# Two waits moved in a two-sweep hybrid decoder block: the attention projection's results and the next sweep's norms

## The chip, the cores and the metric

The kernel runs on one core of a Trainium2 chip. The metric is device time in microseconds (us) of one execution. The core has five engines that work side by side and wait for each other through semaphores: TensorE (PE: matmuls, with its weight loads PEld), VectorE (DVE), ScalarE (ACT), GpSimd (POOL), and SyncE (SP), whose queue issues the transfers. Each engine works its own instructions in the order in which they stand in the program.

## The reference

A decoder block over 2048 tokens of width 1024, in float32:

```python
h = rmsnorm(x, norm_g)
proj = h @ w_in          # glu_in, conv_gate, q, k, v, attn_gate, merge_logits
c = silu(layernorm(depthwise_conv31(a * sigmoid(b))))       # a, b = glu_in
y_conv = (c * silu(conv_gate)) @ w_conv_out
a = sliding_window_attention(rope(q), rope(k), v, sinks)    # window 128, 16 heads, 4 kv heads
y_attn = (a * silu(attn_gate)) @ w_attn_out
merged = sigmoid(m_conv) * y_conv + sigmoid(m_attn) * y_attn
out = rmsnorm(x + merged @ w_out, final_norm_g)
```

## The kernel before

The tokens are worked in two sweeps of 1024, and each product of a sweep in two halves of 512 tokens. The tiles have channels on the 128 partitions and tokens along the row, so a product of 128 output channels and one half is eight steps over the input channels. Each float32 operand is split into a high and a low part, and each step is three matmuls (high x high, high x low, low x high), 24 matmuls for a half. A line over all steps, `Line.run`, calls the products (items) one after another. An item yields after each step, and `spend` then moves a planned clock `t` on and puts in other work that is due: background operations (`bg`, one every `every` us of planned time), and chains (`late`), which are generators that yield the planned us until they may go on. TensorE's order is the order in which the program writes its matmuls. The other engines' orders are set by a scheduler from dependences and priorities, with what is written earlier or at high priority first.

In a sweep the products are, in this order: the inputs of the convolution (`gb`, `ga`), k, v and q, the gates (`ag`, `cg`, `ma`, `mc`, spilled to DRAM), with the attention's small matmuls in between, then:

- `ya`, the attention projection, 8 items of 128 channels (e = 0 to 7) with two halves. A result stands in a bank of PSUM, out of a pool of three banks (`mm_ps`), and VectorE empties it: `ev` in `ya_item` loads the merge gate (`lma`) and multiplies it into the tile `mp`. The tile `mp[e]` lies in the slot `C[e]`, in which the convolution's result `cv[e]` stood. So the operations that read `cv[e]` have to be written before: these are the gated tiles, `u_op(e, h)`, which load the gate (`lcg`), multiply it with `cv[e]` on VectorE (lcg<-lcg,cv, L815), cast the high part on ScalarE (uT<-lcg, L301) and subtract it for the low part on VectorE (uT<-lcg,uT, L234). There are 16 of them, two per channel block. They are background operations, and `u_op` notes each in `stored`.
- `yc`, the convolution's projection, 8 items that read all sixteen uT. VectorE and GpSimd add `mp` to its result, and the sum is split into `mT`.
- `o`, the output product, 16 blocks (n = 0, 1 for the halves of the output channels, b = 0 to 7 for 128 tokens). Beside it, in sweep 0, `prepare` makes the next sweep's input. It squares rows of x on ScalarE (`next_square`), and after blocks 3 and 7 starts a chain, `next_norm`, for the norm of one half of 512 tokens. Its first part makes n10 (for half 0) or n11 (half 1): a root (n11rt), a diagonal tile (n11d) and its high and low part (n11h on ScalarE, n11l on VectorE). After a planned wait, two matmuls by a tile of ones spread the norm over the partitions (n10ms, n11ms), and ScalarE copies the result to `rs`. `next_h` multiplies it with the loaded x (xh) and splits that into `hT`, the input of sweep 1.

The weights of each item come in two parts of four steps (raw_ya, with the number of the item and of the part, 20 and 21 for e = 2). They are cast on ScalarE (whi_ya), GpSimd subtracts for the low part (wlo_ya), and SP stores that to DRAM (d_lo). Four buffers hold each kind.

Of the kernel before, what the change touches and what calls it, by code (L numbers as in the profile page):

```python
# [53 lines left out]
def hybrid_block(ctx: ExitStack, tc: tile.TileContext, x, xt, par_d, w_in, w_conv, sinks, w_attn, w_out,  # L54
# [26 lines left out]
    def slot(tag, shape, dt, name):  # L81
        n = int(np.prod(shape[1:]))
        full = 1024 + P if tag in WIDE else 1024
        t = slots.tile([P, full], dt, tag=tag, name=name)
        v = t[:, 0:n]
        if len(shape) == 3:
            v = v.rearrange("p (a b) -> p a b", b=shape[2])
        elif len(shape) == 4:
            v = v.rearrange("p (a b c) -> p a b c", b=shape[2], c=shape[3])
        return v  # L90

    def t2k(name, dt=F32):
        return work.tile([P, TH], dt, tag="t2k", name=name, bufs=5)
# [65 lines left out]
    class Line:  # L159
# [46 lines left out]
        def finish(self):  # L206
            self.finish_bg()
            while self.late:
                self.t = max(self.t, min(c[0] for c in self.late))
                self.spend(0.1)  # L210

        def run(self, items):


            held = None
            for item in items:
                item[0]()
                if held is not None:
                    for us in held[1]():
                        self.spend(us)  # L220
                held = item
            for us in held[1]():
                self.spend(us)
            self.finish()

    line = Line()
# [6 lines left out]
    def split_lo(out_, full, hi, eng):  # L233
        eng.tensor_tensor(out=out_, in0=full, in1=f(hi), op=ALU.subtract)  # L234
# [38 lines left out]
    def small_bank(name):  # L273
        return tp_ps.tile([P, 4, P], F32, tag="tp", name=name).rearrange("p a b -> p (a b)")

    def project(src, rhs, name, evac, halves=(0, 1), small=False):

        got = {}

        def prefetch():  # L280
            got["w"] = load_w(src, name)

        def blocks():
            for half in halves:
                if small:
                    ps = small_bank(f"mm_{name}{half}")
                else:
                    ps = mm_ps.tile([P, TH], F32, tag="mm", name=f"mm_{name}{half}")
                for k in range(KC):
                    product(ps, got["w"][0](k), rhs(k, half), k)  # L290
                    if k == KC - 1:
                        with tc.high_priority(offset=PRIO):
                            evac(half, ps)
                    if half == halves[-1] and k % 4 == 3:
                        got["w"][1](k // 4)
                    yield 3 * MM_US

        return prefetch, blocks, (src, name, evac)
# [20 lines left out]
    def norm_chain(ss, bank, rs, wait, name):  # L319

        rt = work.tile([P, 2, 4], F32, tag="rt", name=f"{name}rt")
        act.activation(out=rt[:, 0], in_=ss, func=AF.Sqrt, bias=eps, scale=1.0 / D)
        dve.reciprocal(out=rt[:, 1], in_=rt[:, 0])
        dg = t2k(f"{name}d").rearrange("p (b t) -> p b t", t=P)
        dve.tensor_tensor(out=dg, in0=ident.unsqueeze(1).broadcast_to([P, 4, P]),
                          in1=rt[:, 1].unsqueeze(2).broadcast_to([P, 4, P]), op=ALU.mult)
        dg = dg.rearrange("p b t -> p (b t)")
        hi, lo = (t2k(f"{name}{p}", F32R) for p in "hl")
        act.copy(hi, dg)
        split_lo(lo, dg, hi, dve)  # L330
        yield 0.0, wait
        ms = bank()
        for i, part in enumerate((hi, lo)):
            pe.matmul(out=ms, lhsT=ones, rhs=part, start=(i == 0), stop=(i == 1))
        act.activation(out=rs, in_=ms, func=AF.Copy, scale=float(D))
        yield 2 * MM_US, 0.0
# [132 lines left out]
    def sweep(s):  # L469
# [59 lines left out]
        stored = set()  # L529
# [11 lines left out]
        def load_gate(kind, e, half):  # L541
            g = t2k(f"l{kind}{s}_{e}_{half}")
            nc.sync.dma_start(out=g, in_=spill[kind][s * KC + e, :, half * TH:(half + 1) * TH])
            return g
# [297 lines left out]
        def start_u():  # L842
            uT.extend(make_tiles(HT, h, f"uT{s}_") for h in range(2))
# [37 lines left out]
        def ya_item(e, first):  # L881
            def ev(half, ps):
                if half == 0:
                    if ("u", e, 1) not in stored:
                        line.finish()
                    mp[e] = slot(C[e], [P, T], F32, f"mp{s}_{e}")
                g = load_gate("ma", e, half)
                dve.tensor_tensor(out=mp[e][:, half * TH:(half + 1) * TH], in0=ps, in1=g, op=ALU.mult)  # L888

            prefetch, blocks, _ = project(w_attn[e], lambda k, half: aT[half][k],  # L890
                                       f"ya{s}_{e}", ev)
            if not first:
                return prefetch, blocks

            def first_blocks():
                start_u()
                if None in aT[0] + aT[1]:
                    line.finish()
                yield from blocks()

            return prefetch, first_blocks
# [26 lines left out]
        nx = {}  # L928
# [13 lines left out]
        def next_norm(half):  # L942
            ss = nx["ss"]
            dve.tensor_tensor(out=ss[:, 2], in0=ss[:, 0], in1=ss[:, 1], op=ALU.add)
            return norm_chain(ss[:, 2], lambda: small_bank(f"n{s + 1}{half}ms"), nx["rs"][:, half], 6.0,
                              f"n{s + 1}{half}")

        def next_h(half, k):
# [4 lines left out]
        def prepare(n, b):  # L953
            i = n * NB + b
            if i < 8:
                next_square(i)
            if i in (3, 7):
                line.start(next_norm(i // 4))
            if 6 <= i < 10:
                for k in range(2):  # L960
                    next_h(0, 2 * (i - 6) + k)
            if i == 11:
                ht[1] = make_tiles(h_tags[s + 1], 1, f"hT{s + 1}_")
            if 11 <= i < 15:
                for k in range(2):
                    next_h(1, 2 * (i - 11) + k)
# [121 lines left out]
```

## Time and profile before

| | |
|---|---|
| median of 3 runs | 2035.56 us (2034.6 to 2036.1) |
| the profiled execution, its own time | 2036.56 us |
| its span, from the first to the last instruction | 2034.8 us |
| mean granted TensorE clock | 0.994 of full speed |
| busy: TensorE, VectorE, ScalarE, GpSimd | 1999.4, 1337.9, 1031.3, 395.9 us |
| sweep 0: first ya matmul, first matmul of sweep 1 | 748.92, 1034.28 us |

The profile is of one execution. Its rows give start and duration in us, the engine, the line of the kernel, the instruction with output and inputs (buffer numbers left out), how many of them follow each other, and in brackets how long the engine was idle before and which engine or transfer ended that. In a list of waits stand the sum, the number of times and the longest. The granted clock is TensorE's, as a share of full speed.

### The profile page before, as it was taken

The page shows a single profiled execution, that of the slowest core. Times are in us where ns is not written, and L with a number is a line of the kernel's source. Part 1 is how long each engine was busy: PE and PEld are TensorE (multiplying, and loading weights), DVE is VectorE, ACT ScalarE, POOL GpSimd, SP SyncE. Part 2 cuts the span into 40 slices and gives each one's busy share as a digit, 9 for nine tenths or more (in the row PEclk, how much of TensorE's full clock was granted, in tenths as well). Part 3 has the DMA queues.
Part 4 walks back from the last instruction along what each step waited for, and adds up shares of the span by engine and source line. Part 5 has one row for each costly group of instructions (what it writes and reads, how often), then busy time and mean ns, then how long its engine had stood idle before and what let it go on. Part 6 is the DMA issues. An engine that isn't in the chain of part 4 may idle for free.

```text
span 2034.8 us, 27254 instructions
## 1 busy us (share of the span) xinstructions
PE 1999.4 (98%) x9136; PEld 1658.5 (82%) x9136; DVE 1337.9 (66%) x1931; ACT 1031.3 (51%) x2271; POOL 395.9 (19%) x328
## 2 busy tenths in 40 slices
PE   8999999999999997999999999999999999999998
PEld 6788888888888886888788888888888888888887
DVE  6998879988993363123749587699888924441324
ACT  7321677767677362123523225777777774621222
POOL 0344233233323222341001120110111010001200
PEclk9999999999999998999999999999999999999999
DMA  8445645555556746446543466455555578474432
GB/s 292 145 140 177 219 154 171 172 175 171 160 189 225 254 161 206 145 145 222 176 146 133 148 195 197 153 183 173 173 165 173 169 231 267 163 234 147 149 115 83
DMA packets 268699, 361.13 MB, mean 177 GB/s; under 512 B 28432, under 2 KB 126864, under 8 KB 268560
## 3 DMA queue, kind: packets, MB, share of 16 engines
q1 hardware_dynamic: 268560, 359.40, 54.1%
q8 instruction: 72, 1.18, 0.2%
q14 instruction: 67, 0.55, 0.1%
HBM read 239.75 MB, written 119.54 MB: 177 GB/s over the span
## 4 chain that ended last, share of the span: by engine, by line
PE 51%; DVE 1%; DMA 0%; issue 0%; ACT 0%; DVEq 0%; ACTq 0%
PE o L1012 6%; PE mm_ma L271 4%; PE mm_cg L271 4%; PE mm_ag L271 4%; PE mm_gb L271 4%; PE mm_ga L271 4%; PE mm_mc L271 4%; PE mm_yc L271 4%; PE mm_ya L271 4%; PE mm_q_a L271 2%; PE mm_q_b L271 2%; PE sc L668 2%; PE ov L718 1%; PE mm_v L271 1%; PE tpp L698 1%; PE mm_kb L271 1%
## 5 line engine op out<-in xcount | busy, mean ns | idle before, releaser
L492 DVE SCALAR_TENSOR_TENSOR acc<-glu,par,acc 128x1024 f32<-128x1024 f32 x464 | 596.1, 1285 | 6.1
L1012 PE MATMUL o<-wo,mT 128*128 128x512 f32 x768 | 177.4, 393 | 0.0
L271 PE MATMUL mm_ya<-aT,whi_ya 128*128 128x512 f32 x512 | 158.9, 392 | 12.5 <-DVE mp L888 12.5
L1012 PEld LDWEIGHTS o<-wo,mT 128*128 128x128 f32 x768 | 146.2, 190 | 30.7
L271 PE MATMUL mm_ma<-hT,whi_ma 128*128 128x512 f32 x512 | 159.7, 393 | 0.0
L271 PE MATMUL mm_cg<-hT,whi_cg 128*128 128x512 f32 x512 | 159.7, 393 | 0.0
L271 PE MATMUL mm_ag<-hT,whi_ag 128*128 128x512 f32 x512 | 159.4, 393 | 0.0
L271 PE MATMUL mm_mc<-hT,whi_mc 128*128 128x512 f32 x512 | 157.9, 390 | 0.0
L271 PE MATMUL mm_yc<-uT,whi_yc 128*128 128x512 f32 x512 | 157.6, 389 | 0.0
L709 POOL TENSOR_SCALAR_AFFINE_SELECT pc<-pt 128x1024 fp32r<-128x1024 f32 x60 | 65.6, 1094 | 422.5 <-DVE pt L234 413.7
L271 PE MATMUL mm_gb<-hT,whi_gb 128*128 128x512 f32 x448 | 139.2, 392 | 0.0
L271 PE MATMUL mm_ga<-hT,whi_ga 128*128 128x512 f32 x448 | 139.2, 392 | 0.0
L271 PEld LDWEIGHTS mm_ya<-aT,whi_ya 128*128 128x128 f32 x512 | 96.8, 189 | 33.0 <-DVE mp L888 12.9
L271 PEld LDWEIGHTS mm_yc<-uT,whi_yc 128*128 128x128 f32 x512 | 96.1, 188 | 20.0
L271 PEld LDWEIGHTS mm_mc<-hT,whi_mc 128*128 128x128 f32 x512 | 96.0, 188 | 20.0
L271 PEld LDWEIGHTS mm_ag<-hT,whi_ag 128*128 128x128 f32 x512 | 94.2, 188 | 18.2
L271 PEld LDWEIGHTS mm_ma<-hT,whi_ma 128*128 128x128 f32 x512 | 94.1, 188 | 18.2
L271 PEld LDWEIGHTS mm_cg<-hT,whi_cg 128*128 128x128 f32 x512 | 94.0, 188 | 18.2
L688 ACT ACTIVATE ss<-ss,st 128x128 f32<-128x128 f32 x256 | 99.7, 390 | 11.3 <-DVE st L683 10.7
L271 PE MATMUL mm_ya<-aT,wlo_ya 128*128 128x512 f32 x256 | 100.1, 391 | 0.0
L271 PE MATMUL mm_ma<-hT,wlo_ma 128*128 128x512 f32 x256 | 99.9, 390 | 0.0
L271 PE MATMUL mm_cg<-hT,wlo_cg 128*128 128x512 f32 x256 | 99.9, 390 | 0.0
(449 smaller groups left out, 4255.6 us busy)
## 6 DMA issues: line engine op xcount, KB each, us to landing
qk<-d_q SPq DMA_DIRECT2D x256, 64.0 KB, 2.2
d_a<-ss SPq DMA_DIRECT2D x128, 128.0 KB, 1.9
aT<-d_a SPq DMA_DIRECT2D x32, 512.0 KB, 5.9
qk<-d_k SPq DMA_DIRECT2D x240, 64.0 KB, 2.0
raw_ag<-in_w_in_dram SPq DMA_DIRECT2D x32, 256.0 KB, 3.7
d_ag<-ag SPq DMA_DIRECT2D x32, 256.0 KB, 2.2
ss<-d_ag SPq DMA_DIRECT2D x64, 128.0 KB, 2.6
raw_cg<-in_w_in_dram SPq DMA_DIRECT2D x32, 256.0 KB, 3.5
```

The source lines that it names most:

```text
L271: pe.matmul(out=ps, lhsT=a, rhs=b, start=(k == 0 and i == 0), stop=(k == KC - 1 and i == 2))
L492: dve.scalar_tensor_tensor(out=to, in0=glu[c][:, j:j + T], scalar=tap(c, j), in1=acc[c], op0=ALU.mult, op1=ALU.add)
L668: pe.matmul(out=o, lhsT=q[:, h, :], rhs=r, start=(j == 0), stop=(j == 1))
L688: act.activation(out=sb[:, h, :], in_=sb[:, h, :], func=AF.Exp, scale=SCALE, bias=ngm[:, h:h + 1], accum_out=den[:, h:h + 1])
L698: pe.transpose(out=tpp[:, h, :], in_=sb[:, h, :], identity=ident)
L709: pool.affine_select(out=pc, in_=f(pt), pattern=[[0, 2], [0, GQ], [1, P]], compare_op=ALU.is_ge, fill=0.0, base=0, channel_multiplier=-1)
L718: pe.matmul(out=ov, lhsT=vv, rhs=pp[:, i % 2], start=(i == 0), stop=(i == nm - 1))
L1012: pe.matmul(out=ps, lhsT=a[:, c0:c0 + P], rhs=r, start=(k == 0 and i == 0), stop=(k == KC - 1 and i == 2))
```

## The change

There are two edits. In `ya_item`, when the first half of block e is to be emptied and block e's own second gated tile is not written yet, the kernel before writes all background operations and lets all chains end (`finish`). The kernel after writes background operations only until that tile is there (`until`). And the planned wait of the norm chain of the next sweep's halves is 12 us in place of 6.

```diff
         def finish(self):
             self.finish_bg()
             while self.late:
                 self.t = max(self.t, min(c[0] for c in self.late))
                 self.spend(0.1)
+
+        def until(self, ok):
+            while not ok():
+                if self.bg:
+                    self.bg.popleft()()
+                else:
+                    self.t = max(self.t, min(c[0] for c in self.late))
+                    self.spend(0.1)
...
             def ev(half, ps):
                 if half == 0:
-                    if ("u", e, 1) not in stored:
-                        line.finish()
+                    line.until(lambda: ("u", e, 1) in stored)
                     mp[e] = slot(C[e], [P, T], F32, f"mp{s}_{e}")
...
-            return norm_chain(ss[:, 2], lambda: small_bank(f"n{s + 1}{half}ms"), nx["rs"][:, half], 6.0,
+            return norm_chain(ss[:, 2], lambda: small_bank(f"n{s + 1}{half}ms"), nx["rs"][:, half], 12.0,
                               f"n{s + 1}{half}")
```

The lines behind the first edit stand 8 numbers further on in the kernel after, and 7 behind the second. No instruction is added or taken away on any engine. The ya stage of sweep 1 has the same order in both.

VectorE, in sweep 0, where ya begins; a name like uT_1_6 is half 1 of gated tile 6, mp_0<-mm_ya_00 the result of half 0 of item 0. Before, the end of the gated tiles:

```order
L815 TENSOR_TENSOR lcg_6_1_7244<-lcg_6_1_7244,cv_6_5881 128x512
L234 TENSOR_TENSOR uT_0_6_7140<-lcg_6_0_7239,uT_0_6_7140 128x512
L815 TENSOR_TENSOR lcg_7_0_7249<-lcg_7_0_7249,cv_7_6565 128x512
L234 TENSOR_TENSOR uT_1_6_7148<-lcg_6_1_7244,uT_1_6_7148 128x512
L815 TENSOR_TENSOR lcg_7_1_7254<-lcg_7_1_7254,cv_7_6565 128x512
L234 TENSOR_TENSOR uT_0_7_7141<-lcg_7_0_7249,uT_0_7_7141 128x512
L888 TENSOR_TENSOR mp_0_7259<-mm_ya_00_7150,lma_0_0_7260 128x512
L888 TENSOR_TENSOR mp_0_7259<-mm_ya_01_7263,lma_0_1_7289 128x512
L234 TENSOR_TENSOR uT_1_7_7149<-lcg_7_1_7254,uT_1_7_7149 128x512
L888 TENSOR_TENSOR mp_1_7330<-mm_ya_10_7305,lma_1_0_7331 128x512
```

After, the beginning of the gated tiles:

```order
L823 TENSOR_TENSOR lcg_0_1_7184<-lcg_0_1_7184,cv_0_1313 128x512
L242 TENSOR_TENSOR uT_1_0_7142<-lcg_0_1_7184,uT_1_0_7142 128x512
L895 TENSOR_TENSOR mp_0_7189<-mm_ya_00_7150,lma_0_0_7190 128x512
L823 TENSOR_TENSOR lcg_1_0_7197<-lcg_1_0_7197,cv_1_2036 128x512
L823 TENSOR_TENSOR lcg_1_1_7208<-lcg_1_1_7208,cv_1_2036 128x512
L823 TENSOR_TENSOR lcg_2_0_7220<-lcg_2_0_7220,cv_2_2785 128x512
L895 TENSOR_TENSOR mp_0_7189<-mm_ya_01_7193,lma_0_1_7234 128x512
L242 TENSOR_TENSOR uT_0_0_7134<-lcg_0_0_7173,uT_0_0_7134 128x512
```

The mp of the first half moved from behind 31 of the 32 operations of the gated tiles to behind three of them. After the second mp stand 9 operations of gated tiles, then the third mp, then 7, the fourth, 8, the fifth, 2, the sixth.

ScalarE, at the same place, after the change; whi_ya_30 and whi_ya_31 are the two parts of item 3's weights, which stand behind all uT casts before:

```order
L309 CAST uT_1_2_7144<-lcg_2_1_7238 128x512
L309 CAST uT_0_3_7137<-lcg_3_0_7262 128x512
L309 CAST uT_1_3_7145<-lcg_3_1_7273 128x512
L257 CAST whi_ya_30_7350<-raw_ya_30_7349 128x512
L309 CAST uT_0_4_7138<-lcg_4_0_7287 128x512
L309 CAST uT_1_4_7146<-lcg_4_1_7303 128x512
L309 CAST uT_0_5_7139<-lcg_5_0_7314 128x512
L257 CAST whi_ya_31_7356<-raw_ya_31_7355 128x512
```

The weight casts moved between the casts of the gated tiles.

TensorE, in sweep 0's output product, second half of the channels (o_1_1 is n = 1, block 1). Before:

```order
L1012 MATMUL o_1_0_8851<-wo_1_7_8817,mT_0_7_7834 128x512 x3
L1012 MATMUL o_1_1_8895<-wo_1_0_8761,mT_0_0_7827 128x512 x3
L334 MATMUL n11ms<-n11h,ones 128x512
L334 MATMUL n11ms<-n11l,ones 128x512
L1012 MATMUL o_1_1_8895<-wo_1_1_8769,mT_0_1_7828 128x512 x3
```

After:

```order
L1019 MATMUL o_1_1_8895<-wo_1_7_8817,mT_0_7_7834 128x512 x3
L1019 MATMUL o_1_2_8939<-wo_1_0_8761,mT_0_0_7827 128x512 x3
L1019 MATMUL o_1_2_8939<-wo_1_1_8769,mT_0_1_7828 128x512 x3
L342 MATMUL n11ms<-n11h,ones 128x512
L342 MATMUL n11ms<-n11l,ones 128x512
L1019 MATMUL o_1_2_8939<-wo_1_2_8777,mT_0_2_7829 128x512 x3
```

The pair n11ms moved back by nine steps of o, 27 matmuls. The pair n10ms moved by the same number, from behind the first step of block 5 (n = 0) to behind the second step of block 6.

## The prediction

> **What bounds the kernel now.** I read the page's head first, then the waits of TensorE, then the chain that ended last, and then the timelines around the waits.
>
> ```profile
> span 2034.8 us, 27254 instructions
> ...
> PE 1999.4 (98%) x9136; PEld 1658.5 (82%) x9136; DVE 1337.9 (66%) x1931; ACT 1031.3 (51%) x2271; POOL 395.9 (19%) x328
> ```
>
> TensorE is the bound. Only time in which it stands still, or runs slowly, can be won. The waits of TensorE, sorted by size:
>
> ```profile
> PE mm_ya L271 <- DVE mp L888: 12.5, 1, 12.5
> PE mm_gb L271 <- ACT w L249: 6.9, 1, 6.9
> PE n11ms L334 <- ACT n11h L329: 3.9, 1, 3.9
> ...
> PE n11ms L334 <- DVE n11l L234: 0.7, 1, 0.7
> ...
> PE n10ms L334 <- DVE n10l L234: 0.2, 1, 0.2
> ```
>
> The wait of 6.9 is the start of the kernel, which the change leaves alone. The other four rows, 12.5 + 3.9 + 0.7 + 0.2 = 17.3 us, belong to the two edits. No row names a product of sweep 1. Idle time is not the whole price, though. The chain that ended last gives the pace of sweep 1, and the start of its first product:
>
> ```profile
> 1034.28 10.88 PE mm_gb L271 x48
> ...
> 1767.02 87.04 PE mm_ya L271 x384
> 1854.06 87.04 PE mm_yc L271 x384
> 1941.10 87.05 PE o L1012 x384
> ```
>
> In sweep 1 ya, yc and o take 87.04 + 87.04 + 87.05 = 261.13 us for 1152 matmuls, 0.2267 each, 5.44 us for a half of 24. Sweep 0 runs the same 1152 and the four of the two norms (0.91 us) between its first ya matmul and 1034.28. TensorE's timeline has that first matmul and the long wait:
>
> ```profile
> 748.92 0.61 PE L271 MATMUL mm_ya<-aT,whi_ya 128*128 128x512 f32 x2
> ...
> 765.01 0.39 PE L271 MATMUL mm_ya<-aT,wlo_ya 128*128 128x512 f32 x1
> 777.91 1.22 PE L271 MATMUL mm_ya<-aT,whi_ya 128*128 128x512 f32 x2 [12.51 <-DVE mp L888]
> ...
> 782.27 0.62 PE L271 MATMUL mm_ya<-aT,whi_ya 128*128 128x512 f32 x2
> ```
>
> So sweep 0 needs 1034.28 - 748.92 = 285.36 us where 261.13 + 0.91 = 262.04 would do: 23.3 us are lost, 6 more than the idle rows say. The stretches show why (columns: TensorE, its weight loads, VectorE, ScalarE, GpSimd busy, granted clock, DMA share, GB/s):
>
> ```profile
> 765.24:777.91 12.67, 0.16 (x1) 0.00 (x1) 12.50 (x17) 6.07 (x11) 3.14 (x2) 0.59 0.81 258
> 777.91:782.50 4.59, 4.59 (x14) 3.65 (x14) 1.93 (x3) 0.22 (x1) 0.00 (x0) 0.65 0.92 309
> 782.50:850.50 68.00, 68.00 (x301) 56.31 (x300) 8.32 (x13) 8.08 (x14) 16.75 (x13) 1.00 0.44 151
> ...
> 988.00:994.20 6.20, 1.55 (x5) 0.77 (x4) 6.14 (x13) 4.40 (x10) 0.00 (x0) 0.89 0.92 329
> 994.20:1001.00 6.80, 6.80 (x20) 5.33 (x19) 5.02 (x8) 1.91 (x4) 0.00 (x0) 0.60 0.47 152
> 1001.00:1034.28 33.28, 33.28 (x148) 27.57 (x147) 20.32 (x35) 12.41 (x29) 0.35 (x2) 1.00 0.45 156
> ```
>
> After each long wait the granted clock is 0.65 and 0.60 for some microseconds, then 1.00. TensorE is busy there and yet behind. From 777.91 to 782.27 it starts 12 matmuls in 4.36 us instead of 2.72.
>
> **The change part by part.** It removes and adds no instruction. It moves VectorE, ScalarE and SP instructions in sweep 0's ya stage, and two pairs of matmuls in sweep 0's output stage.
>
> First edit, ya in sweep 0. There are three banks for products, so half number i+3 of ya cannot start before the mp product has emptied the bank of half i. In the order before, the mp of half 0 stands behind all gated tiles but one. VectorE's timeline:
>
> ```profile
> 751.74 1.89 DVE L815 TENSOR_TENSOR lcg<-lcg,cv 128x512 f32<-128x512 f32 x3
> 754.11 1.29 DVE L234 TENSOR_TENSOR uT<-lcg,uT 128x512 fp32r<-128x512 f32 x2 [0.49 <-ACT uT L301]
> ...
> 758.02 4.09 DVE L234 TENSOR_TENSOR uT<-lcg,uT 128x512 fp32r<-128x512 f32 x3
> ...
> 775.85 0.68 DVE L815 TENSOR_TENSOR lcg<-lcg,cv 128x512 f32<-128x512 f32 x1
> 776.45 0.68 DVE L234 TENSOR_TENSOR uT<-lcg,uT 128x512 fp32r<-128x512 f32 x1
> 777.17 0.69 DVE L888 TENSOR_TENSOR mp<-mm_ya,lma 128x512 f32<-128x512 f32 x1
> ```
>
> Half 0 was complete at 748.92 + 5.44 = 754.36, and its mp ran at 777.17. Half 3 was due at 748.92 + 3 x 5.44 = 765.24 and started at 777.91: 12.67 us, and 4.36 - 2.72 = 1.64 at the low clock, 14.3 in all.
>
> The new order puts the mp of half 0 behind three instructions, and the others between groups of gated tiles. I walk it at 0.60 us a step (775.85 to 776.45). Dear steps: uT beside GpSimd's wlo took 4.09 for three, 2.2 more than 1.8, and GpSimd's rows coincide with them:
>
> ```profile
> 758.51 3.05 POOL L234 TENSOR_TENSOR wlo_ya<-raw_ya,whi_ya 128x512 fp32r<-128x512 f32 x2 [18.46 <-ACT whi_ya L249]
> 766.65 3.14 POOL L234 TENSOR_TENSOR wlo_ya<-raw_ya,whi_ya 128x512 fp32r<-128x512 f32 x2 [5.09 <-DMA d_lo<-wlo_ya]
> ```
>
> Each pair of wlo thus costs VectorE up to 2.2 us, and three pairs fall into the stretch. Half i ends at 754.36 + 5.44 i, and I add 0.2 for the signal. mp 0: 754.6 + 0.6 = 755.2, due 765.24. Three lcg, then mp 1, which waits for its half: 760.0 + 0.6 = 760.6, due 770.68. Nine steps, 5.4 (with two pairs 9.8), and 0.6 for mp 2 itself: 766.6 to 771.0, due 776.12. Seven steps, 4.2 (with half a pair 5.3): mp 3 at 771.5 to 776.9, due 781.56. Eight steps, 4.8 (5.9): mp 4 at 776.9 to 783.4, due 787.00. Two steps: mp 5 at 782.4 to 785.2, due 792.44. Every mp is in time, by 3.6 us in the dear column and by 9.5 or more in the cheap one. TensorE does not wait: 14.3 us won.
>
> What the new waits hold up: VectorE now stands before each mp until its half is done, with lcg and uT queued behind. The last uT comes at some 778 to 785 instead of 779.6. Its reader is yc, due at 748.92 + 87.04 = 835.96: no cost, 50 us of cover. On ScalarE the weight casts stand between uT casts. The cast of block 3's first weights follows uT_1_3, some 767 to 772. It could not be before half 3 is half done anyway, 768.0, as it was at 782.28 before:
>
> ```profile
> 782.28 0.62 ACT L249 CAST whi_ya<-raw_ya 128x512 fp32r<-128x512 f32 x1 [5.10 <-PE mm_ya L271]
> ```
>
> With GpSimd's 1.5 us behind it the weights are there by 774 at the latest, due 781.56. On SP the loads of lma move ahead, and two stores of wlo (blocks 2) stand before the loads of the last eight lcg. They wait for GpSimd until some 766. I cost this at nothing, since the eight lcg are due from 769 on. If that cover is gone, an mp is late by what exceeds 3.6 us.
>
> In sweep 1 the order of ya is the same in both programs: nothing.
>
> Second edit, the norms. Each pair now stands 27 matmuls further back, 27 x 0.2267 = 6.12 us. The rows of n11:
>
> ```profile
> 983.67 4.70 PE L1012 MATMUL o<-wo,mT 128*128 128x512 f32 x20
> 992.30 0.50 PE L334 MATMUL n11ms<-n11h,ones 128*128 128x512 f32 x1 [3.93 <-ACT n11h L329]
> 993.52 0.79 PE L334 MATMUL n11ms<-n11l,ones 128*128 128x512 f32 x1 [0.72 <-DVE n11l L234]
> ```
>
> and VectorE's last step before them:
>
> ```profile
> 992.79 0.68 DVE L234 TENSOR_TENSOR n11l<-n11d,n11h 128x512 fp32r<-128x512 f32 x1
> ```
>
> TensorE was there at 983.67 + 20 x 0.2267 = 988.2. It will come at 994.3 on the same scale, and n11l is complete at 993.47: 0.8 us to spare. VectorE's new order also takes one hT (about 0.7) from ahead of n11l. n10 waited 0.2 and gets 6.12: to spare. What goes is the rest of the loss, 23.3 - 14.3 = 9.0 us: 0.2 + 3.9 + 0.7 idle, and 4.2 of low clock and slow steps around them (20 recorded matmuls in 6.80 us instead of 4.5, and the pair itself).
>
> What a late norm makes late is the next sweep's hT, half 1:
>
> ```profile
> 995.34 0.59 ACT L335 ACTIVATE rs<-n11ms 128x512 f32<-128x512 f32 x1
> ...
> 1015.84 0.73 DVE L340 SCALAR_TENSOR_TENSOR hT<-xh,par,hT 128x512 fp32r<-128x512 f32 x1
> ```
>
> From rs to the last hT it takes 21.2 us. The new rs comes at 994.3 + 1.4 = 995.7 on the scale that had n11 at 988.2, so hT is complete at 1016.9. On that scale gb of sweep 1 begins 8.1 earlier than 1034.28, at about 1026, and its half 1 at 1031.6: 15 us of cover.
>
> The price of the low clock could also be taken from the Trainium skill, page "TensorE: Matmul & The Clock Gate", Part 1: after an idle window of about 3.4 us the array runs at half rate and needs about 3.4 us of activity to be released. By it each of the two long waits would cost about 1.7 us more, and the sum would be 17.3 + 3.4 = 20.7, a time near 2015. The trace agrees at ya (1.64), and at n11, with 0.60 over 6.8 us, it shows more than one such window. I keep the trace's sum.
>
> Sum: -14.3 - 9.0 = -23.3, and I give back 0.3 for short waits that may stay at n10 and n11. The profiled execution took 2036.56 (span 2034.8, 1.7 around it), so it would be 2013.5. The median of the runs, 2035.56, lies 1.0 lower: 2012.5.
>
> **The rivals.** First, n11 stays partly. Its 0.8 us to spare is thin, and xh and xs loads stand ahead of it on VectorE. If they are 1 to 5 us late, 0.2 to 4 us come back, with the low clock up to 7: 2013 to 2019.5. For it speaks the thin margin, against it the hT that is gone from ahead.
>
> Second, VectorE stays behind TensorE in ya: at 1.36 a step (4.09 for three) the 13 uT between mp 1 and mp 4 cost 9.9 us more than at 0.60, and mp 4 ends at 786.8, just in time. Any lcg load that is late behind SP's stores, by the 3 us that such a load takes or by twice that, then stops TensorE for 3 to 6 us: 2015 to 2019. For it speaks that VectorE has some 28 us of work in 30 us there, against it that only six wlo run in the stretch.
>
> Third, slower: sweep 1 waits for hT, since rs of half 1 comes later against the start of sweep 1. It decides once that chain of 21.2 us grows by more than its 15 us of cover. It must grow by 38 us to eat the gain too. At 42 us more the time would be 2040. Nothing in the rows stretches it so far.
>
> Fourth, the change does nothing that counts, 2035.5: the order of sweep 0 speaks against it.
>
> **How the numbers follow.** Both waits gone 0.80 (2011 to 2014), n11 partly 0.08, ya partly 0.08, slower 0.02, nothing 0.02. The range 2010.5 to 2017 takes the first case, with 1.5 us of spread between runs (2034.6 to 2036.1), and most of the next two. About 0.2%, 4 us, is what a measurement here can tell from no change: faster 0.96, same 0.02, slower 0.02.
>
> **What would show it.** Right: no wait of mm_ya for mp and none of n11ms among TensorE's waits; mp of half 0 some 6 us after the first ya matmul; granted clock 1.00 from 749 to the end; gb of sweep 1 starting near 1011; last uT before 786. Wrong: a wait of mm_ya for mp or for wlo_ya of blocks 2 to 4, a wait of n11ms of over 1 us, or a first wait of sweep 1's gb for hT.

## The result, and the profile after

The kernel after takes 2012.85 us, the median of 4 runs (2012.16 to 2013.28), the kernel before beside it 2035.54 (2034.60 to 2036.10). The ratio is 0.9889, with a 95% interval from 0.9872 to 0.9906: 22.7 us less, where 2012.5 was forecast. The head of the page:

```profile
span 2011.6 us, 27250 instructions
...
PE 1993.1 (99%) x9136; PEld 1654.8 (82%) x9136; DVE 1337.0 (66%) x1931; ACT 1031.6 (51%) x2271; POOL 396.8 (20%) x328
```

The span is 23.2 us shorter, and TensorE is busy for only 6.3 us less: 17 us were idle time, the rest was slow time that counted as busy. Each engine has the same number of instructions as before. Of the waits of TensorE the four rows of before are gone, and none stands in their place. The two longest are now the start of the kernel and one in the attention:

```profile
PE mm_gb L279 <- ACT w L257: 7.2, 1, 7.2
PE sc L676 <- DVE pt L242: 1.3, 1, 1.3
```

The chain that ended last is now TensorE alone from ya to the next sweep:

```profile
748.92 87.04 PE mm_ya L279 x384
835.96 87.04 PE mm_yc L279 x384
923.00 34.01 PE o L1019 x150
957.00 0.46 PE n10ms L342 x2
957.46 21.81 PE o L1019 x96
979.27 0.46 PE n11ms L342 x2
979.73 31.32 PE o L1019 x138
1011.05 10.88 PE mm_gb L279 x48
```

Sweep 0 now has sweep 1's pace, 87.04 us for ya. The stretches of after (columns as before) cover ya, the place of the old wait, and the output product:

```profile
748.75:835.79 87.04, 87.04 (x385) 72.07 (x384) 36.22 (x50) 28.30 (x42) 23.77 (x17) 1.00 0.59 200
765.24:777.91 12.67, 12.67 (x57) 10.49 (x57) 11.80 (x17) 5.37 (x9) 3.09 (x2) 1.00 0.82 268
...
922.83:1011.05 88.22, 88.22 (x390) 72.98 (x389) 50.49 (x87) 44.14 (x106) 1.64 (x3) 1.00 0.59 203
```

Where the kernel before stood for 12.5 us, TensorE works all 12.67 us with the clock at 1.00. VectorE works 11.80 there, 12.50 before: the same work, in another order. The two starts that split the loss of before are these, from TensorE's timeline of before:

```profile
850.27 0.62 PE L271 MATMUL mm_yc<-uT,whi_yc 128*128 128x512 f32 x2
...
937.32 7.87 PE L1012 MATMUL o<-wo,mT 128*128 128x512 f32 x34
```

Before, ya took 850.27 - 748.92 = 101.35 us, after 87.04: 14.31 won. The output product took 1034.28 - 937.32 = 96.96, after 88.22: 8.74 won. Together 23.05.

VectorE's mp, in the timeline of after:

```profile
754.67 0.69 DVE L895 TENSOR_TENSOR mp<-mm_ya,lma 128x512 f32<-128x512 f32 x1
...
759.83 0.69 DVE L895 TENSOR_TENSOR mp<-mm_ya,lma 128x512 f32<-128x512 f32 x1 [1.21 <-PE mm_ya L279]
760.44 3.58 DVE L242 TENSOR_TENSOR uT<-lcg,uT 128x512 fp32r<-128x512 f32 x4
765.97 1.34 DVE L823 TENSOR_TENSOR lcg<-lcg,cv 128x512 f32<-128x512 f32 x2 [1.94 <-DMA lcg<-d_cg]
...
769.26 0.69 DVE L895 TENSOR_TENSOR mp<-mm_ya,lma 128x512 f32<-128x512 f32 x1
...
775.34 0.68 DVE L895 TENSOR_TENSOR mp<-mm_ya,lma 128x512 f32<-128x512 f32 x1
...
781.75 0.69 DVE L895 TENSOR_TENSOR mp<-mm_ya,lma 128x512 f32<-128x512 f32 x1
782.36 1.28 DVE L242 TENSOR_TENSOR uT<-lcg,uT 128x512 fp32r<-128x512 f32 x2
783.56 0.68 DVE L895 TENSOR_TENSOR mp<-mm_ya,lma 128x512 f32<-128x512 f32 x1
787.03 0.69 DVE L895 TENSOR_TENSOR mp<-mm_ya,lma 128x512 f32<-128x512 f32 x1 [2.79 <-PE mm_ya L279]
```

The bracket of the last row is the sign that VectorE has caught up: it now waits for TensorE (2.79 us).

### The profile page after: what moved, and what is told of

Same layout as the page of the kernel before. It is cut to its first block, busy times and chain, and to the rows that moved or that the text cites. A ratio compares the mean times of both kernels' runs of the same rounds, so it can differ in the third digit from the quotient of the medians.

```text
span 2011.6 us, 27250 instructions
## 1 busy us (share of the span) xinstructions
PE 1993.1 (99%) x9136; PEld 1654.8 (82%) x9136; DVE 1337.0 (66%) x1931; ACT 1031.6 (51%) x2271; POOL 396.8 (20%) x328
## 4 chain that ended last, share of the span: by engine, by line
PE 91%; DVE 7%; ACT 1%; issue 0%; DMA 0%; DVEq 0%; SPq 0%; ACTq 0%
PE mm_ma L279 9%; PE mm_mc L279 9%; PE o L1019 9%; PE mm_ya L279 9%; PE mm_yc L279 9%; PE mm_ga L279 8%; PE mm_gb L279 8%; PE mm_cg L279 8%; PE mm_ag L279 5%; PE mm_q_a L279 4%; PE mm_q_b L279 4%; DVE acc L500 4%; PE sc L676 3%; PE ov L726 2%; PE mm_v L279 2%; PE tpp L706 1%
## 5 line engine op out<-in xcount | busy, mean ns | idle before, releaser
L279 PE MATMUL mm_ag<-hT,wlo_ag 128*128 128x512 f32 x256 | 99.9, 390 | 0.0
```

The lines of the kernel that those rows point to most:

```text
L279: pe.matmul(out=ps, lhsT=a, rhs=b, start=(k == 0 and i == 0), stop=(k == KC - 1 and i == 2))
```

## The experiments

Eight kernels were run, seven made from the kernel after and e_norm from the kernel before. In both series some executions of a kernel took some 5 to 7 us more than others of the same kernel; the kernel before stood at 2034.5 to 2037.2 in one group and 2040.2 to 2044.2 in the other. Two profiled executions, those of e_norm and e_fill2, show a wait of TensorE of 4.2 to 4.3 us ahead of ya, to which the last section comes; whether the other long executions had the same wait, no trace tells. So each experiment is read by its own stage, from the first ya matmul to the first gb matmul of sweep 1, with its times beside it. At full pace the stage takes 262.04. The ya column is from the timeline and the gb column from the chain, which dates gb 0.16 us later than the timeline does, in every kernel; so 262.30 is full pace to within 0.1 us, and the differences between kernels are not touched.

| kernel | ya in sweep 0 | gb in sweep 1 | stage |
|---|---|---|---|
| before | 748.92 | 1034.28 | 285.36 |
| after | 748.75 | 1011.05 | 262.30 |
| e_until: first edit alone | 748.39 | 1017.75 | 269.36 |
| e_norm: second edit alone | 753.57 | 1031.57 | 278.00 |
| e_fill: first edit, 76 small matmuls ahead of n11ms | 747.73 | 1019.24 | 271.51 |
| e_fill2: the same with 40 | 752.97 | 1020.91 | 267.94 |
| e_w8: after, norm wait 8 | 749.04 | 1015.05 | 266.01 |
| e_w20: after, wait of n11 20 | 748.25 | 1010.55 | 262.30 |
| e_k3: after, mp behind 3 further blocks | 749.26 | 1016.66 | 267.40 |
| e_k4: after, mp behind 4 further blocks | 749.10 | 1018.87 | 269.77 |

**Each edit alone.** In e_until the norm's wait is 6 again; e_norm is the kernel before with the wait at 12, so that `ev` calls `finish` as before.

```diff
 e_until, against the kernel after
-            ... nx["rs"][:, half], 12.0,
+            ... nx["rs"][:, half], 6.0,
 e_norm, against the kernel before
-            ... nx["rs"][:, half], 6.0,
+            ... nx["rs"][:, half], 12.0,
```

> Changed kernel with the norms' planned wait back at 6 (only the first edit is left). Theory (each wait costs its idle time and the low clock behind it, and the two places do not touch each other): 2035.5 - 14.3 = 2021.2 us; the wait of mm_ya is gone, n11ms still waits 4.7 us, with a granted clock of about 0.6 for some 7 us behind it. Rival (the gain is shared, sweep 1 or the output stage takes up part of it, or n11 needs the first edit as well): off from 2021.2 by 2 us or more.

> Kernel before with the norms' planned wait at 12 (only the second edit). Theory: 2035.5 - 9.0 = 2026.5 us; n10ms and n11ms do not wait, mm_ya still waits 12.5 us for mp. Rival (the low clock behind n11 comes from something else, such as the transfers that are busiest there): only the idle 4.9 us go, 2030.6.

e_until: median 2021.32 (2020.12, 2020.25, 2022.38, 2027.51), ratio 0.9924 (0.9901 to 0.9948). e_norm: median 2033.97 of 10 runs, 4 of them at 2027.06 to 2029.09 and 6 at 2033.9 to 2035.1; the profiled one is among these and has the wait ahead of ya; ratio 0.9963 (0.9948 to 0.9979). So e_norm's median missed the 2026.5 that was expected, and only the quicker four come near it, 0.6 to 2.6 us above. TensorE's longest wait in e_until, from ya on (0.7 and 0.3 follow, for n11l and n10l):

```profile
PE n11ms L342 <- ACT n11h L337: 3.7, 1, 3.7
```

and in the timeline of e_norm:

```profile
782.69 1.22 PE L271 MATMUL mm_ya<-aT,whi_ya 128*128 128x512 f32 x2 [12.64 <-DVE mp L888]
```

Each edit takes away its own wait and leaves the other whole. The stages give 285.36 - 269.36 = 16.0 for the first and 285.36 - 278.00 = 7.4 for the second: 23.4, against 23.06 for both. By parts it is closer still: ya takes 835.43 - 748.39 = 87.04 in e_until, and the output product 1031.57 - 943.35 = 88.22 in e_norm, each as in after. What differs is the price of the wait that is left: the output product took 95.28 in e_until and 96.96 in before, ya 102.74 in e_norm and 101.35 in before. Nothing that the one edit wins is lost through the other, and the rival's 2030.6 for e_norm (idle time only) does not stand.

**Is it the idle time that lowers the clock, or the transfers beside it?** The low clock after n11 coincides with a DMA share of 0.92 ahead of it. e_fill leaves the norm's wait at 6 and gives TensorE matmuls in place of the idle time, which write to the bank that n11ms overwrites. e_fill2 has 40 in place of 76.

```diff
+        if name == "n11":
+            for _ in range(76):
+                pe.matmul(out=ms[:, 0:P], lhsT=ones, rhs=ones, start=True, stop=True)
```

> As the kernel with only the first edit, with 76 matmuls of 128 columns (ones by ones, into the bank that n11ms overwrites) put ahead of n11ms, so that TensorE is busy for about 4.5 us of its wait; they are extra work. Theory (idle TensorE draws the low clock): granted clock stays at 1.00 behind n11ms, the o matmuls there take 0.227 each, and of the 9.0 us of the norms some 3 go: 2018.2 us. Rival (the slow matmuls behind the wait come from the transfers, DMA share 0.9 there, or from the wait itself): still 20 matmuls in 6.8 us behind n11ms, 2021.2 or more.

Median 2021.99 (2021.64 to 2022.54), ratio 0.9922 (0.9904 to 0.9940). The chains, first of e_until, then of e_fill:

```profile
978.40 0.80 PE n11ms L342
979.20 38.55 PE o L1019 x165
```

```profile
972.86 8.44 PE n11ms L343 x76
...
981.81 37.43 PE o L1022 x165
```

The same 165 matmuls take 38.55 us behind a wait and 37.43 behind the filler, which is full pace (165 x 0.2267 = 37.41). The stretches of e_fill:

```profile
972.00:976.00 4.00, 4.00 (x35) 3.86 (x33) 4.00 (x10) 3.66 (x9) 0.00 (x0) 1.00 1.00 351
976.00:980.00 4.00, 4.00 (x38) 4.00 (x38) 2.64 (x6) 1.84 (x5) 0.00 (x0) 1.00 0.72 246
```

With the DMA engines busy all the time (1.00) the clock stays at 1.00. So the slow stretch belongs to TensorE's idle time. The time itself missed the 2018.2 that was expected and lies where the rival had it, since a filler cost 8.44 / 76 = 0.111 us, twice what I had taken, and stood beyond the norm's arrival.

> As the kernel with the first edit alone and filler matmuls ahead of n11ms (extra work), but 40 of them: 76 took 8.6 us, 0.113 each, and ended 4 us after n11h. 40 take 4.5 us and end about when n11l is ready. Theory (an idle TensorE draws the low clock): clock 1.00 behind n11ms, the 165 o matmuls behind it in 37.4 us instead of 38.6 with the first edit alone, the pair itself at full pace, and 1.5 to 2.5 us less than the first edit alone in time. Rival (transfers or the wait itself make the slow matmuls): the same time as the first edit alone, and a stretch of low clock.

e_fill2: 2023.35, 2025.97, 2024.26 and 2017.48, median 2023.81, ratio 0.9923 (0.9892 to 0.9953). Its profiled execution had the wait ahead of ya. Its stage, 267.94, is 1.4 less than e_until's: the 40 fillers fill the wait of 4.4 us and no more, and 165 o matmuls then take 37.45. Against 2021.3 for e_until the expected 1.5 to 2.5 us less would be 2018.8 to 2019.8; one run of four lies below that and three above, so the time alone settles nothing here. The stage agrees in direction, and the 165 matmuls at full pace agree with e_fill.

**How little idle time lowers the clock.** e_w8 sets the wait so that TensorE comes to n11 a little too early (12.0 becomes 8.0).

> Changed kernel with the norms' planned wait at 8 instead of 12: n11ms stands 9 matmuls (2.0 us) behind its place in the kernel before. n11l is ready 10.3 to 11.4 us after the output product's second part starts, TensorE comes at 8.2: a wait of 2.2 to 3.2 us. Theory a (a wait of under some 3.4 us draws no low clock, as the rule of the Trainium skill's page on TensorE and the clock gate has it): 2012.9 + 2.7 = 2015.6, granted clock 1.00 behind it. Theory b (low clock behind any wait of 2 us or more): 2017 to 2018.5, with a stretch at about 0.6.

2017.63, 2022.23, 2016.14 and 2016.68, median 2017.15, ratio 0.9904 (0.9877 to 0.9930). TensorE's timeline:

```profile
976.40 0.51 PE L342 MATMUL n11ms<-n11h,ones 128*128 128x512 f32 x1 [0.92 <-ACT n11h L337]
977.56 0.50 PE L342 MATMUL n11ms<-n11l,ones 128*128 128x512 f32 x1 [0.66 <-DVE n11l L242]
```

and the stretches behind it:

```profile
976.40:978.06 1.66, 1.00 (x3) 0.64 (x4) 1.66 (x4) 1.26 (x3) 0.00 (x0) 1.00 0.95 333
978.06:980.00 1.94, 1.94 (x7) 1.53 (x7) 1.94 (x6) 1.39 (x3) 0.00 (x0) 0.66 0.21 67
980.00:982.00 2.00, 2.00 (x7) 1.54 (x6) 1.47 (x2) 0.62 (x1) 0.00 (x0) 0.50 0.46 140
982.00:984.00 2.00, 2.00 (x10) 1.68 (x9) 1.57 (x3) 0.72 (x2) 0.00 (x0) 0.98 0.95 320
```

Behind 1.58 us of idle time in two pieces (0.92 + 0.66) the clock falls to 0.50 and is back after some 3.4 us (an estimate from these rows: 1.94 x 0.34 / 0.50 = 1.3 in the second, 2.0 in the third, 0.1 in the fourth). The stage is 3.7 us longer than after's, more than twice the idle time, and the time is theory b's, though the wait came out shorter than expected. Not every short wait does this: e_k3 (below) has a wait of 0.90 us with the clock at 1.00 over the 5.7 us behind it, and one of 1.29 us in after's attention (at 340.21) has it at 1.00 over the next 9.8. The Trainium skill, page "TensorE: Matmul & The Clock Gate", Part 1, lets the array fall back only after a window of about 3.4 us of idle time. No such window is in this trace, so here the measurement decides against that sentence of the page.

**Does a later norm cost anything?** This is the place of the rival that ends slower. e_w20 puts n11ms 36 matmuls further back.

```diff
-            ... nx["rs"][:, half], 12.0,
+            ... nx["rs"][:, half], 20.0 if half else 12.0,
```

> Changed kernel with the planned wait of the second norm (n11) at 20 instead of 12: n11ms stands 36 matmuls, 8.2 us, further back, so that rs and the hT of half 1 come later, closer to the start of sweep 1. Theory (hT of half 1 has some 16 us of cover, and is held by the o products before it anyway): 2012.9, the first gb and ga of sweep 1 do not wait. Rival (the cover is gone): gb of half 1 waits for hT, up to 8 us more.

2012.97, 2013.15, 2019.74 and 2011.61, median 2013.06, ratio 0.9882 (0.9857 to 0.9908), the stage 262.30 as in after. TensorE's timeline, then VectorE's with the last hT:

```profile
986.77 0.39 PE L342 MATMUL n11ms<-n11h,ones 128*128 128x512 f32 x1
```

```profile
1002.90 0.75 DVE L348 SCALAR_TENSOR_TENSOR hT<-xh,par,hT 128x512 fp32r<-128x512 f32 x1 [0.78 <-ACT hT L347]
```

The pair comes 7.7 us later than in after, hT only 3.3 us later, and its first reader, gb's half 1 at 1010.55 + 5.44 = 1015.99, is still 12.3 us away. So the cover held, and the time is the 2012.9 that was expected.

**How far back may mp stand?** e_k3 and e_k4 let background operations run further ahead before mp, to find the point at which a wait comes back.

```diff
-                    line.until(lambda: ("u", e, 1) in stored)
+                    line.until(lambda: ("u", min(e + 3, KC - 1), 1) in stored)    # e_k4: e + 4
```

> Changed kernel in which the first half of block e waits in the order for the gated tiles up to block e+3 (until tile min(e+3, 7) is written): the mp of half 0 stands behind 15 of the 32 gated-tile operations. Theory (what counts is whether mp of half 0 is done before half 3 of ya is due, 16.3 us after ya begins): mp ends some 16 us after ya begins, a wait of 0 to 1.5 us, with low clock behind it if there is one: 2013 to 2016. Rival (each operation ahead of mp costs): half of the 14.3 us comes back, 2020.

> As the kernel before in this list, but up to block e+4: mp of half 0 stands behind 21 operations. Theory: VectorE reaches it some 21.5 us after ya begins (lcg_5_0 began at 770.26 in the kernel before), half 3 is 5.5 to 6.5 us late, with 1.6 us of low clock behind it: 2012.9 + 7.6 = 2020.5. Rival (something else than mp's place, such as the weights' casts or the transfers, made the wait of 12.5 us): no wait of mm_ya for mp, or all of it, 2013 or 2027.

e_k3: median 2020.26 (2017.18 to 2023.93), ratio 0.9912 (0.9889 to 0.9935). e_k4: median 2031.03 (2026.0 to 2034.13, 9 runs), ratio 0.9966 (0.9953 to 0.9979). TensorE's timeline of e_k3:

```profile
772.08 0.70 PE L279 MATMUL mm_ya<-aT,whi_ya 128*128 128x512 f32 x2 [0.90 <-ACT uT L309]
...
779.79 0.73 PE L279 MATMUL mm_ya<-aT,whi_ya 128*128 128x512 f32 x2 [1.98 <-DVE mp L895]
```

and of e_k4:

```profile
771.41 1.22 PE L279 MATMUL mm_ya<-aT,whi_ya 128*128 128x512 f32 x2 [5.78 <-DVE mp L895]
...
1772.11 1.22 PE L279 MATMUL mm_ya<-aT,whi_ya 128*128 128x512 f32 x2 [4.19 <-DVE mp L895]
```

In e_k4 the mp of half 0 comes too late, and the wait of 5.78 and the stage, 7.5 us longer than after's, are what was expected of sweep 0; neither case of the rival, no wait or all of it, came. The time is 2031.03 where 2020.5 was expected. What I had left out is sweep 1, whose order this edit changes too: half 3 waits 4.19 us there, and from gb on the kernel takes 2026.6 - 1018.87 = 1007.7 us against after's 2011.6 - 1011.05 = 1000.6. The two together are 14.6 of the 15.0 us by which its profiled execution, 2028.30, lies above after's. In e_k3 the mp of half 0 is in time, as expected, yet 2.9 us of waits come back at halves 4 and 5, the clock is at 0.69 and 0.50 for 4.2 us behind the second, and sweep 1 takes 1.5 us more (2018.8 - 1016.66 = 1002.1). So 2013 to 2016 was missed, and 2020.26 is the number of the rival. The row of 0.90 names a uT of ScalarE, but the mp of the bank that half 4 needs ended at the same moment (771.26 + 0.68 = 771.94). I had worked out the first mp alone; the later ones stand behind the same backlog. (In the traces 14 and 20 operations of gated tiles stand ahead of the first mp, not 15 and 21.) So the first edit's gain comes from the place of the mp in VectorE's queue, and the waits come back in steps as that place moves back: 0, 2.9, 5.8 and 12.5 us of idle time in sweep 0 for after, e_k3, e_k4 and before.

## Why the prediction was right

- **The first term, 14.3.** ya went from 101.35 to 87.04: 14.31.
- **The second term, 9.0.** The output product went from 96.96 to 88.22: 8.74. The sum, 23.05, is near the 23.0 that was forecast partly by luck: the 0.3 given back was for short waits, and none stayed; but of the 23.3 some 0.16 were no loss, only the two datings of gb.
- **The split between idle and slow time.** It holds for the profiled execution only. The wait of ya cost 101.35 - 87.04 - 12.51 = 1.8 beyond its idle time in before. In e_norm, ya took 856.31 - 753.57 = 102.74 us with 12.64 idle, so 3.1 beyond it. The same wait thus has a price that differs by 1.3 us. The Trainium skill, page "TensorE: Matmul & The Clock Gate", Part 1, calls the window in which activity is counted free-running, so that the same kernel's slow time differs from run to run. The traces agree that the price differs; that such a window is the reason, no run here shows. The estimate from that page (about 1.7 us for each long wait, a time near 2015) came out 2 us too high, because n11 cost 8.74 - 4.85 = 3.9 beyond its idle time in before (in e_until it was 7.06 - 4.7 = 2.4).
- **The walk of mp.** The mp end at 755.4, 760.5, 770.0, 776.0, 782.4 and 784.2, where 755.2, 760.6, 766.6 to 771.0, 771.5 to 776.9, 776.9 to 783.4 and 782.4 to 785.2 were forecast. From the third on they lie near the dear ends: the uT beside GpSimd took 3.58 for four, and VectorE waited 1.94 us for a load of lcg, a term that the forecast had put at nothing. The tightest was 4.4 us in time (mp 4, 782.44, due 786.83). The rival of a VectorE that stays behind needed that same kind of late load and had it, once; it lacked the size. e_k3 shows the edge: there TensorE waits.
- **The norm.** n11l was there at 976.53 + 0.68 = 977.21, and TensorE came at 979.11, so 1.9 us were to spare where 0.8 was forecast:

```profile
979.11 0.39 PE L342 MATMUL n11ms<-n11h,ones 128*128 128x512 f32 x1
```

```profile
976.53 0.68 DVE L242 TENSOR_TENSOR n11l<-n11d,n11h 128x512 fp32r<-128x512 f32 x1
...
999.58 0.75 DVE L348 SCALAR_TENSOR_TENSOR hT<-xh,par,hT 128x512 fp32r<-128x512 f32 x1 [0.50 <-ACT hT L347]
```

  The rival "n11 stays partly" was rightly priced, as e_w8 shows: 1.58 us of waits gave 2017.15, inside its 2013 to 2019.5. It did not come, by 1.9 us.
- **The slower rival.** ScalarE made rs at 982.04, 2.9 us behind the pair where 1.4 was taken, since the output's own work stood ahead. hT was complete at 1000.3 for a gb half due at 1016.5: 16 us of cover, 15 forecast.
- **What was to be seen.** No wait of mm_ya or n11ms, mp of half 0 5.9 us after the first ya matmul, clock 1.00 in the stretches, gb at 1011.05 (near 1011), the last uT at 783.6 (before 786).

## What to carry to other kernels

Look for work that stands in an engine's queue ahead of the operation that frees a buffer, when its own reader is tens of microseconds away: only what the freed slot really needs has to come first. Walk every reuse of the buffer and not the first alone, and every loop pass in which the order changes. When a tensor engine is the bound, price a wait by the time of the whole stage against an undisturbed pass of the same work, since a wait can cost more than its idle time.

## What the runs showed of the hardware that was not expected

Two things stand above: 1.58 us of idle time in two pieces were enough to lower the clock to 0.50 for some 3.4 us, where single waits of 0.90 and 1.29 us left it at 1.00, and a matmul of 128 columns in a row of its like cost 0.111 us against 0.2267 for 512 columns.

The third is the wait ahead of ya in e_norm and e_fill2. GpSimd's timeline, first of e_norm, which had it, then of after, which had not:

```profile
701.90 14.39 POOL L234 TENSOR_TENSOR wlo_mc<-raw_mc,whi_mc 128x512 fp32r<-128x512 f32 x3 [8.83 <-ACT whi_mc L249]
```

```profile
703.07 1.40 POOL L242 TENSOR_TENSOR wlo_mc<-raw_mc,whi_mc 128x512 fp32r<-128x512 f32 x1 [8.83 <-ACT whi_mc L257]
704.80 1.90 POOL L242 TENSOR_TENSOR wlo_mc<-raw_mc,whi_mc 128x512 fp32r<-128x512 f32 x1 [0.34 <-ACT whi_mc L257]
```

Three wlo take 14.39 us in the one, two take 1.40 and 1.90 in the other. VectorE runs without a gap from 697 to 712.6 in e_norm. Its rows beside the start of GpSimd, of e_norm and of after:

```profile
702.06 2.36 DVE L766 TENSOR_TENSOR cv<-cv,mu 128x1024 f32<-128x1024 f32 x2
```

```profile
703.24 4.55 DVE L774 TENSOR_TENSOR cv<-cv,mu 128x1024 f32<-128x1024 f32 x2
```

In after it is VectorE that takes 4.55 us instead of 2.36. The two programs have the same order here. What decides which engine gives way stays open: GpSimd's first wlo starts 0.16 us ahead of VectorE's row in e_norm and 0.17 us ahead in after. SP's queue shows how long GpSimd was out. The first store of these wlo, in e_norm and in after:

```profile
713.82 0.33 SPq L265 DMA_DIRECT2D d_lo<-wlo_mc  x1
```

```profile
704.50 0.33 SPq L273 DMA_DIRECT2D d_lo<-wlo_mc  x1
```

In e_norm even the first wlo was done only at some 713.8, 1.2 us after VectorE's row had ended. What follows there is a chain of queues: SP's store of mc stands behind those of wlo, ScalarE waits for the landing of the mc store, and TensorE for ScalarE. ScalarE's row and TensorE's:

```profile
720.42 1.15 ACT L775 ACTIVATE sq<-cv 128x512 f32<-128x512 f32 x2 [8.71 <-DMA d_mc<-mc]
```

```profile
723.66 1.12 PE L271 MATMUL mm_mc<-hT,whi_mc 128*128 128x512 f32 x2 [4.27 <-ACT mc L534]
```

The Trainium skill, page "SBUF — State Buffer", section "Who interferes with whom", says that VectorE and GpSimd share a pair of ports of the on-chip memory (SBUF) as an exclusive lock, and that a VectorE instruction with two inputs there contends with a GpSimd instruction that reads there. The rows agree that one engine stands while the other works. In e_norm GpSimd stays out over a whole row of VectorE's instructions; why, stays open. This reading was not tried by an experiment: it rests on the profiles of e_norm and e_fill2, which both show 14.39 us for three, against the eight others, in which VectorE's pair takes 4.55 or 4.56 us and no mm_mc waits for ScalarE.
